# A hybrid decoder trunk on one core: how the second mixer's attention is ordered on TensorE

## The chip, the cores and the metric

One core of one Trainium2 chip runs the whole program. The metric is the device time of one execution in microseconds (us); three runs of the kernel before gave 1995.99 to 1997.3, the median is 1996.11.

## The reference, cut to what matters

Two layers, each a token mixer, a layer norm, a channel mixer of experts (PEER), a layer norm and a gate. Layer 0 mixes with an SSD, layer 1 with causal attention. The sequence has 256 tokens and one key block of 256, so the block selection of the reference selects nothing and what is left is plain causal attention with a linear position term, 16 heads of 64:

```python
logit_own = (jnp.einsum('hqd,hkd->hqk', qb, k_own).astype(f32) * scale
             - slopes[:, None, None] * dist[None])
logit_own = jnp.where((o_pos[None, :] <= t[:, None])[None], logit_own, -jnp.inf)
...
probs = jax.nn.softmax(
    jnp.concatenate([logit_sel.reshape(H, MOBA_Q_BLOCK, n_sel), logit_own], axis=-1), axis=-1)
...
        + jnp.einsum('hqk,hkd->hqd', p_own, v_own))
```

Its output goes through `w_out`, then `x = layer_norm(alpha * x + mix, ...)`, then the experts.

## The kernel before, in words

Four stages follow each other: `ssd`, `peer(0)`, `moba`, `peer(1)`. The change is in `moba` alone (and in two helpers).

Two kinds of matmul appear. **Dense** ones are products with weights. A weight chunk of 512 KB is loaded by SP's queue into `raw`, ACT casts a high part (line 113) and DVE subtracts to get a low part (line 114, `split`); `chunk` does the three. `mm3` (line 138) then issues three matmuls in the rounded format for each tile. `stationary` makes a query or key block: 8 tiles, 24 matmuls of 256 columns. `moving` makes the output projection: per chunk two halves of the tokens, 12 matmuls of 512 columns. There are four buffers for raw and four for split chunks. **Plain** ones are full fp32 matmuls: scores, transposes, values.

PSUM has three pools: `mm` (2 banks, queries and keys), `acc` (4 banks, long accumulations) and `aux` (2 banks, all the small things).

`moba` loops over eight head pairs. `query(j)` (line 558) and `key(j)` (565) make 128 rows for the two heads of pair j, head 0 on partitions 0 to 63, head 1 on 64 to 127. ACT copies the query into `qz`, a buffer per head that is zero on the other head's partitions (lines 539, 540, 563), so that a score matmul (line 583) can run over all 128 partitions of the key. Then, in `attend`:

- `scores(h2)`: two matmuls per head, for the two token blocks (128 and 256 keys); DVE adds the position term (line 586) and takes the maxima (588);
- `weights`: DVE scales the maxima (591), ACT takes four exponentials with their sums (595), DVE the reciprocals (597);
- `turn(h2)`: DVE normalises (603), PE transposes three 128x128 blocks (605), ACT copies them to SBUF (607);
- `values`: per head three matmuls onto 64 rows of the output, that is on 64 columns of the array (615 to 617); `split` stores the result for the output projection.

`out` projects earlier pairs' results from pair 3 on. The last matmuls, the two layer norms and a projection of the per-layer input follow in `end_mixer`. There the layer norm's first DVE operation (line 182) needs the projected values of pair 7.

**The order.** The program is traced in Python order, and the framework then orders each engine's instructions: by program order among those that are ready in its own estimate, so later dense matmuls move ahead of attention steps that are still waiting. `weave` (line 40) sets the program order: main steps (query and key of the next pair, an output chunk) with side steps (the attention) between them. `after(marks)` keeps what is traced in it behind given instructions on the same engine; `pace.marks` are the load and the two split halves of the latest chunk. Each engine then runs its list in order.

The lines that the prediction speaks of are 113, 114 (splits), 138 (dense matmuls), 173 (the layer norm's transposes), 196 (its last DVE step), 563, 569 (copies of query and key), 583 to 617 (attention).

Of the kernel before, what the change touches and what calls it, by code (L numbers as in the profile page):

```python
# [7 lines left out]
F32 = mybir.dt.float32  # L8
# [4 lines left out]
OP = mybir.AluOpType  # L13
AX = mybir.AxisListType.X
# [3 lines left out]
P = 128  # L18
T = 256
D = 1024  # L20
KD = D // P
# [36 lines left out]
class Net:  # L58
# [76 lines left out]

    def mm3(self, out, lhs, rhs, start, stop):
        for i, (a, b) in enumerate(SPLIT):
            self.nc.tensor.matmul(out, lhs(a), rhs(b), start=start and i == 0, stop=stop and i == 2)  # L138

    def stationary(self, out, hl, m=P):  # L140
        for k in range(KD):
            self.mm3(out, lambda a: hl[:, a, k * m:(k + 1) * m], lambda b: self.xT[:, b, k, :],
                     k == 0, k == KD - 1)

    def halves(self, out, hl):
        o = out.rearrange("p (b t) -> p b t", b=2)
# [386 lines left out]
    def moba(self):  # L533
        nc, dram = self.nc, self.dram
        with self.tc.tile_pool(name="moba", bufs=1) as pool:
            self.pool = pool
            alibi = pool.tile([P, 2, T], F32, name="alibi")
            v = pool.tile([P, 2, D], F32, name="v")
            qz = pool.tile([P, 2, 2, T], F32, name="qz")
            nc.gpsimd.memset(qz, 0.0)  # L540
            at = {}
            ks = {}

            def value(h):
                if h == 0:
                    acc, hls = self.head
                    for kp in range(4):
                        self.moving(acc[1], hls[kp], self.xk(kp, 1), kp == 0, kp == 3)
                else:
                    acc = [self.acc() for _ in range(2)]  # L550
                    for kp in range(4):
                        hl = self.chunk(dram["w_v"][h * 4 + kp])
                        for tb in range(2):
                            self.moving(acc[tb], hl, self.xk(kp, tb), kp == 0, kp == 3)
                for tb in range(2):
                    nc.scalar.copy(v[:, tb, h * 512:(h + 1) * 512], acc[tb])

            def query(j):
                pq = self.mm()
                self.stationary(pq[:, :T], self.chunk(dram["w_qk"][2 * j]))  # L560
                for h2 in range(2):
                    r = slice(64 * h2, 64 * h2 + 64)
                    nc.scalar.copy(qz[r, j % 2, h2, :], pq[r, :T])

            def key(j):
                pk = self.mm()
                self.stationary(pk[:, :T], self.chunk(dram["w_qk"][2 * j + 1]))
                ks[j] = self.tl([P, T], "k", 2)
                nc.scalar.copy(ks[j], pk[:, :T])

            def attend(j):
                s = {}

                def scores(h2):
                    if h2 == 0:
                        s["lg"] = self.tl([P, 2, 2, T], "lg", 2)
                        s["mx"] = self.tl([P, 2, 2], "mx", 2)
                        s["sm"] = self.tl([P, 2, 2], "sm", 2)
                    slope = 2.0 ** (-8.0 * (2 * j + h2 + 1) / 16)
                    psc = self.aux().rearrange("p (b s) -> p b s", b=2)  # L580
                    for tb in range(2):
                        w = (tb + 1) * P
                        nc.tensor.matmul(psc[:, tb, :w], qz[:, j % 2, h2, tb * P:w], ks[j][:, :w], start=True, stop=True)
                    for tb in range(2):
                        w = (tb + 1) * P
                        nc.vector.scalar_tensor_tensor(s["lg"][:, h2, tb, :w], alibi[:, tb, :w], 8.0 * slope,
                                                       psc[:, tb, :w], op0=OP.mult, op1=OP.add)
                        nc.vector.tensor_reduce(s["mx"][:, h2, tb:tb + 1], s["lg"][:, h2, tb, :w], AX, OP.max)

                def weights():  # L590
                    nc.vector.tensor_scalar(s["mx"], s["mx"], -0.125, None, op0=OP.mult)
                    for h2 in range(2):
                        for tb in range(2):
                            l = s["lg"][:, h2, tb, :(tb + 1) * P]
                            nc.scalar.activation(l, l, AF.Exp, bias=s["mx"][:, h2, tb:tb + 1], scale=0.125,
                                                 accum_out=s["sm"][:, h2, tb:tb + 1])
                    nc.vector.reciprocal(s["sm"], s["sm"])

                def turn(h2):
                    pt = self.aux()[:, :384].rearrange("p (b t) -> p b t", b=3)  # L600
                    for tb in range(2):
                        l = s["lg"][:, h2, tb, :(tb + 1) * P]
                        nc.vector.tensor_scalar(l, l, s["sm"][:, h2, tb:tb + 1], None, op0=OP.mult)
                    for b, (tb, sb) in enumerate(((0, 0), (1, 0), (1, 1))):
                        nc.tensor.transpose(pt[:, b, :], s["lg"][:, h2, tb, sb * P:(sb + 1) * P], self.ident)
                    s["pt", h2] = self.tl([P, 3, P], "pt", 3)
                    nc.scalar.copy(s["pt", h2], pt)

                def values():
                    po = self.aux()[:, :T].rearrange("p (b t) -> p b t", b=2)  # L610
                    for h2 in range(2):
                        r = slice(64 * h2, 64 * h2 + 64)
                        cs = slice(j * P + 64 * h2, j * P + 64 * h2 + 64)
                        pt = s["pt", h2]
                        nc.tensor.matmul(po[r, 0], v[:, 0, cs], pt[:, 0], start=True, stop=True)
                        nc.tensor.matmul(po[r, 1], v[:, 0, cs], pt[:, 1], start=True, stop=False)
                        nc.tensor.matmul(po[r, 1], v[:, 1, cs], pt[:, 2], start=False, stop=True)
                    if j % 2 == 0:
                        at[j // 2] = self.tl([P, 2, 2, T], "at", 2, F32R)
                    a = at[j // 2]  # L620
                    self.split(a[:, 0, j % 2], a[:, 1, j % 2], po.rearrange("p b t -> p (b t)"))

                return [lambda: scores(0), lambda: scores(1), weights, lambda: turn(0), lambda: turn(1), values]

            lhs = lambda kp, tb: lambda a, k: at[kp][:, a, k, tb * P:(tb + 1) * P]
            last = []

            def out(kp, h):
                hl = self.chunk(dram["w_mo"][kp * 2 + h])
                if kp >= 2:  # L630
                    last.append((h, kp, hl))
                    return
                for tb in range(2):
                    self.moving(oacc[tb][h], hl, lhs(kp, tb), kp == 0, False)

            value(0)
            with self.after(self.pace.marks):
                nc.sync.dma_start(alibi, dram["consts"][:, C_ALIBI:].rearrange("p (b s) -> p b s", b=2))
            value(1)
            query(0)  # L640
            key(0)
            oacc = self.accs()
            for j in range(8):
                main = []
                if j < 7:
                    main += [lambda: query(j + 1), lambda: key(j + 1)]
                if j >= 3:
                    kp, h = divmod(j - 3, 2)
                    main.append(lambda: out(kp, h))
                self.weave(main, attend(j))  # L650
                if j == 4:
                    gb = pool.tile([P, 2, D], F32, tag="ac", bufs=4, name="gb")
                    with self.after(self.pace.marks):
                        self.load_gb(gb, 2)
                        x = pool.tile([P, 2, D], F32, name="x")
                        nc.sync.dma_start(x, self.x_m)
                if j == 6:
                    self.ple_load(1, pool)
            out(2, 1)
            out(3, 0)  # L660
            out(3, 1)
            dump = pool.tile([P, D], F32, tag="lg", bufs=2, name="dump")
            self.end_mixer(1, oacc, x, gb, dump, pool, last, lhs)
# [398 lines left out]
```

## Time and profile before

| | before |
|---|---|
| median of 3 runs | 1996.11 us |
| the profiled execution | 1996.32 us, span 1994.4 us |
| TensorE busy | 1977.0 us, 99% of the span |
| VectorE, ScalarE busy | 78%, 57% |
| TensorE clock | full speed in all of the 40 slices |

The profile is of one execution. A busy share counts time in which an engine has an instruction running; matmuls overlap at their ends, so what a stretch of them costs is best read from the start of one group to the start of the next in the timeline. There a row gives the start, the duration, the engine, the line, the operation, the tiles and the number of merged instructions. An fp32 matmul shows as two MATMUL records (a transpose as one).

### The profile page before, as it was taken

Reading aid. Unit: us, or ns where it says so; the run is one execution under the profiler, and the core shown is the slowest. Engines: PE = TensorE matmul, PEld = TensorE weight load, DVE = VectorE, ACT = ScalarE, POOL = GpSimd, SP = SyncE. Lnnn points to the kernel's source line nnn. Section 1 sums busy time; section 2 is a strip of 40 time slices with the busy share of each in tenths; the row PEclk is TensorE's granted clock in tenths of the full one; section 3 lists DMA queues with packets and bytes.
Section 4 is the critical chain, followed back from the end, with each engine's and each line's share of the span. In section 5 each row is a group of like instructions: output and inputs, shape, how many; then the busy total and the mean of one; then the engine's idle time right before and its main releaser. Section 6 shows DMA issues by size and latency. Waiting matters only on the chain.

```text
span 1994.4 us, 33756 instructions
## 1 busy us (share of the span) xinstructions
PE 1977.0 (99%) x12658; PEld 1706.0 (86%) x12658; DVE 1549.8 (78%) x3050; ACT 1138.1 (57%) x1920; POOL 135.4 (7%) x159
## 2 busy tenths in 40 slices
PE   9999999999999999999999999999999999999999
PEld 8988898888888888888889889888888888888887
DVE  8786658998888998866765665899887889886675
ACT  7754556677556444445635645667756554445563
POOL 0001001111111000000000000111111100000000
PEclk9999999999999999999999999999999999999999
DMA  7446668888787545666735455888877755566672
GB/s 285 159 137 212 209 183 231 225 221 244 215 217 211 186 167 179 229 213 205 247 134 208 143 188 175 235 226 216 242 217 220 213 187 174 169 221 223 203 250 65
DMA packets 121155, 403.01 MB, mean 202 GB/s; under 512 B 13440, under 2 KB 14368, under 8 KB 119328
## 3 DMA queue, kind: packets, MB, share of 16 engines
q1 hardware_dynamic: 102560, 367.29, 55.4%
q0 software_dynamic: 18432, 33.56, 9.9%
q8 instruction: 100, 1.64, 0.3%
q14 instruction: 63, 0.52, 0.1%
HBM read 360.92 MB, written 6.32 MB: 184 GB/s over the span
## 4 chain that ended last, share of the span: by engine, by line
PE 85%; issue 7%; DVE 5%; ACT 2%; POOL 1%; DMA 1%; SPq 0%; POOLq 0%; ACTq 0%; DVEq 0%
PE acc L138 38%; PE acc L149 21%; PE acc L150 11%; PE mm L138 8%; PE aux L848 3%; DVE hl L114 1%; PE aux L696 1%; PE mm L378 1%; ACT hl L113 0%; PE aux L463 0%; PE mm L173 0%; DVE act L732 0%; PE mm L291 0%; DVE act L733 0%; DVE act L735 0%
## 5 line engine op out<-in xcount | busy, mean ns | idle before, releaser
L114 DVE TENSOR_TENSOR hl<-raw,hl 128x1024 fp32r<-128x1024 f32 x624 | 757.8, 1220 | 246.9 <-ACT hl L113 243.1
L149 PE MATMUL acc<-xT,hl 128*128 128x512 f32 x2048 | 722.4, 397 | 0.0
L138 PE MATMUL acc<-hl,w 128*128 128x512 f32 x3024 | 695.4, 391 | 0.0
L113 ACT CAST hl<-raw 128x1024 fp32r<-128x1024 f32 x626 | 658.3, 1054 | 39.5 <-PE acc L138 17.8
L138 PEld LDWEIGHTS acc<-hl,w 128*128 128x128 f32 x3024 | 565.5, 188 | 116.4
L150 PE MATMUL acc<-xT,hl 128*128 128x256 f32 x2048 | 573.9, 280 | 0.4 <-DVE hl L114 0.4
L149 PEld LDWEIGHTS acc<-xT,hl 128*128 128x128 f32 x2048 | 384.8, 188 | 88.6
L150 PEld LDWEIGHTS acc<-xT,hl 128*128 128x128 f32 x2048 | 387.4, 189 | 1.1 <-DVE hl L114 1.1
L113 ACT CAST w<-act 128x256 fp32r<-128x256 f32 x252 | 102.2, 407 | 344.5 <-PE acc L138 344.4
L138 PE MATMUL mm<-xT,hl 128*128 128x256 f32 x1968 | 256.4, 287 | 0.8 <-DVE xT L114 0.7
L138 PEld LDWEIGHTS mm<-xT,hl 128*128 128x128 f32 x1968 | 242.3, 192 | 5.0 <-issue 2.3
L814 ACT COPY act<-acc 128x256 f32<-128x256 f32 x256 | 96.2, 376 | 254.2 <-PE acc L150 254.2
L114 DVE TENSOR_TENSOR w<-act,w 128x256 fp32r<-128x256 f32 x252 | 106.7, 423 | 78.5 <-ACT w L113 78.2
L818 POOL DMA_DIRECT2D act<-low x128 | 110.5, 863 | 758.5 <-ACT low L815 619.4
L855 DVE SCALAR_TENSOR_TENSOR act<-aux,act 128x256 f32<-128x256 f32 x256 | 90.7, 417 | 9.9 <-PE aux L848 9.9
L815 ACT COPY low<-acc 128x256 f32<-128x256 f32 x256 | 98.2, 384 | 0.0
L839 DVE TENSOR_TENSOR a<-oh,r 128x512 f16<-128x512 f16 x256 | 96.5, 419 | 0.0
L833 DVE TENSOR_TENSOR oh<-iota,r 128x1024 f16<-128x1024 f16 x128 | 87.5, 684 | 0.0
L848 PEld LDWEIGHTS <-oh 128*128 128x128 f16 x2048 | 63.3, 98 | 13.4 <-issue 13.4
L848 PE MATMUL aux<-a,oh 128*128 128x64 f16 x2048 | 70.9, 194 | 0.0
L805 ACT ACTIVATE act<-act 128x1024 f32<-128x1024 f32 x64 | 69.0, 1078 | 0.8 <-DMA act<-low 0.8
L193 POOL TENSOR_TENSOR ln_s<-ln_s,mhalf 128x1 f32<-128x1 f32 x8 | 4.4, 549 | 874.3 <-DVE ln_s L192 874.3
(220 smaller groups left out, 1336.0 us busy)
## 6 DMA issues: line engine op xcount, KB each, us to landing
raw<-in_u SPq DMA_DIRECT2D x256, 512.0 KB, 4.4
raw<-in_v SPq DMA_DIRECT2D x256, 512.0 KB, 4.3
act<-low POOLq DMA_DIRECT2D x128, 256.0 KB, 5.5
raw<-in_w_q SPq DMA_DIRECT2D x32, 512.0 KB, 4.4
raw<-in_w_xbc SPq DMA_DIRECT2D x24, 512.0 KB, 4.3
raw<-in_w_z SPq DMA_DIRECT2D x16, 512.0 KB, 3.3
raw<-in_w_so SPq DMA_DIRECT2D x16, 512.0 KB, 3.4
raw<-in_w_pg SPq DMA_DIRECT2D x16, 512.0 KB, 4.6
```

The source lines that it names most:

```text
L113: a = self.nc.scalar.copy(hi, src)
L114: b = (lo_on or self.nc.vector).tensor_tensor(lo, src, hi.bitcast(F32), op=OP.subtract)
L138: self.nc.tensor.matmul(out, lhs(a), rhs(b), start=start and i == 0, stop=stop and i == 2)
L149: self.nc.tensor.matmul(o, hl[:, 0, c], self.xT[:, :, k, :], start=k == 0, stop=False)
L150: self.nc.tensor.matmul(out[:, :T], hl[:, 1, c], self.xT[:, 0, k, :], start=False, stop=k == KD - 1)
L814: nc.scalar.copy(act[e // 32][:, e % 32, :], pe[:, :T])
L815: copied = nc.scalar.copy(cur["low"][:, e % 2, :], pe[:, T:]).ins
L818: nc.gpsimd.dma_start(both, cur["low"], accum_op=OP.add)
L833: nc.vector.tensor_tensor(pairs(oh2), every(self.iota, P), twins(i2T, P), op=OP.is_equal)
L839: nc.vector.tensor_tensor(pairs(a2[:, k]), pairs(oh1), twins(g2[:, k], 64), op=OP.mult)
L848: nc.tensor.matmul(pg[:, t, :], oh2[:, t], a2[:, k, t], start=k == 0, stop=k == 1)
L855: nc.vector.scalar_tensor_tensor(v, pg[:, :, 32 * a:32 * a + 32].rearrange("p t e -> p e t"), 2.0 ** -12, v, op0=OP.mult, op1=OP.mult)
```

## The change

Order and shape of the attention steps. The query is no longer padded with zeros: one copy of 128 partitions, and a score matmul runs over the 64 partitions of its head, with the two heads alternating. Scores of both heads go into two auxiliary banks at once. The normalising of both heads becomes one `tensor_tensor` per token block. The six transposes stand together: five of them are held behind the first. The values stand together, heads alternating, in a bank of `mm`, and the next pair's scores are held behind the last of them. The second half of a query's matmuls (at pair 6, which has no query left, an output chunk) is held behind the transposes. Queries run two pairs ahead, keys one.

```diff
-    def stationary(self, out, hl, m=P):
+    def stationary(self, out, hl, m=P, late=()):
         for k in range(KD):
-            self.mm3(out, lambda a: hl[:, a, k * m:(k + 1) * m], lambda b: self.xT[:, b, k, :],
-                     k == 0, k == KD - 1)
+            with self.after(late if k >= KD // 2 else ()):
+                self.mm3(out, lambda a: hl[:, a, k * m:(k + 1) * m], lambda b: self.xT[:, b, k, :],
+                         k == 0, k == KD - 1)
...
-            qz = pool.tile([P, 2, 2, T], F32, name="qz")
-            nc.gpsimd.memset(qz, 0.0)
+            qs = {}
...
-            def query(j):
+            def query(j, late=()):
                 pq = self.mm()
-                self.stationary(pq[:, :T], self.chunk(dram["w_qk"][2 * j]))
-                for h2 in range(2):
-                    r = slice(64 * h2, 64 * h2 + 64)
-                    nc.scalar.copy(qz[r, j % 2, h2, :], pq[r, :T])
+                self.stationary(pq[:, :T], self.chunk(dram["w_qk"][2 * j]), late=late)
+                qs[j] = self.tl([P, T], "q", 2)
+                nc.scalar.copy(qs[j], pq[:, :T])
...
-                    for tb in range(2):
-                        w = (tb + 1) * P
-                        nc.tensor.matmul(psc[:, tb, :w], qz[:, j % 2, h2, tb * P:w], ks[j][:, :w], start=True, stop=True)
...
+                    psc = [self.aux().rearrange("p (b s) -> p b s", b=2) for _ in range(2)]
+                    with self.after(held):
+                        for tb in range(2):
+                            w = (tb + 1) * P
+                            for h2 in range(2):
+                                r = slice(64 * h2, 64 * h2 + 64)
+                                nc.tensor.matmul(psc[h2][:, tb, :w], qs[j][r, tb * P:w], ks[j][r, :w], start=True, stop=True)
...
                     for tb in range(2):
-                        l = s["lg"][:, h2, tb, :(tb + 1) * P]
-                        nc.vector.tensor_scalar(l, l, s["sm"][:, h2, tb:tb + 1], None, op0=OP.mult)
...
+                        l = s["lg"][:, :, tb, :(tb + 1) * P]
+                        nc.vector.tensor_tensor(l, l, s["sm"][:, :, tb, None].to_broadcast([P, 2, (tb + 1) * P]), op=OP.mult)
+
+                def turns():
+                    pt = [self.aux()[:, :384].rearrange("p (b t) -> p b t", b=3) for _ in range(2)]
+                    held = ()
+                    for h2, b in ((0, 2), (0, 1), (0, 0), (1, 2), (1, 1), (1, 0)):
+                        tb, sb = (b + 1) // 2, b // 2
+                        with self.after(held):
+                            ins = nc.tensor.transpose(pt[h2][:, b, :], s["lg"][:, h2, tb, sb * P:(sb + 1) * P], self.ident).ins
+                        held = held or (ins,)
...
+                    return (ins,)
+
+                def close(then):
+                    po = self.mm()[:, :T].rearrange("p (b t) -> p b t", b=2)
+                    held = ()
+                    for n, (tb, sb) in enumerate(((0, 0), (1, 0), (1, 1))):
+                        for h2 in (1, 0):
...
+                            with self.after(held):
+                                ins = nc.tensor.matmul(po[r, tb], v[:, sb, cs], s["pt", h2][:, n], start=sb == 0, stop=sb == tb).ins
+                            held = held or (ins,)
...
+                    then((ins,))
...
+            heads = [attend(j) for j in range(8)]
+            heads[0][0](())
+            query(1)
             for j in range(8):
-                main = []
                 if j < 7:
-                    main += [lambda: query(j + 1), lambda: key(j + 1)]
+                    key(j + 1)
+                with self.after(self.pace.marks):
+                    heads[j][1]()
+                    turned = heads[j][2]()
                 if j >= 3:
-                    kp, h = divmod(j - 3, 2)
-                    main.append(lambda: out(kp, h))
-                self.weave(main, attend(j))
+                    out(*divmod(j - 3, 2), late=turned if j >= 6 else ())
+                if j < 6:
+                    query(j + 2, turned)
+                with self.after(self.pace.marks):
+                    heads[j][3](heads[j + 1][0] if j < 7 else lambda held: None)
```

## Rows read from the trace of the kernel before

**Rows 1.** The page, part 1: busy us, share of the span, instructions of each engine.
```profile
PE 1977.0 (99%) x12658; PEld 1706.0 (86%) x12658; DVE 1549.8 (78%) x3050; ACT 1138.1 (57%) x1920; POOL 135.4 (7%) x159
```

**Rows 2.** Windows, first values to last values: PE, PEld, DVE, ACT, POOL busy, clock, DMA share, GB/s.
```profile
1081.12:1153.82 72.70, 71.89 (x506) 63.55 (x506) 49.94 (x125) 45.02 (x113) 0.00 (x0) 1.00 0.49 171
```

**Rows 3.** PE's timeline after the mixer: start, us, instructions, idle before and releaser.
```profile
1163.61 0.65 PE L173 MATMUL mm<-ident,x 128*128 128x128 f32 x4 [2.06 <-DVE x L196]
```

**Rows 4.** PE's timeline, end of pair 4 to pair 6.
```profile
1124.07 1.48 PE L583 MATMUL aux<-k,qz 128*128 128x128 f32 x8
1125.20 3.23 PE L138 MATMUL mm<-xT,hl 128*128 128x256 f32 x24
1128.26 2.94 PE L138 MATMUL acc<-hl,at 128*128 128x512 f32 x12
1131.03 0.40 PE L138 MATMUL mm<-xT,hl 128*128 128x256 f32 x2
1131.56 0.33 PE L605 MATMUL aux<-ident,lg 128*128 128x128 f32 x1
...
1132.47 1.31 PE L138 MATMUL mm<-xT,hl 128*128 128x256 f32 x9
1133.71 0.43 PE L615 MATMUL aux<-pt,v 128*64 128x128 f32 x2
1133.98 0.27 PE L616 MATMUL aux<-pt,v 128*64 128x128 f32 x1
1133.99 0.32 PE L615 MATMUL aux<-pt,v 128*64 128x128 f32 x1
...
1134.47 0.38 PE L617 MATMUL aux<-pt,v 128*64 128x128 f32 x2
1134.79 1.58 PE L138 MATMUL mm<-xT,hl 128*128 128x256 f32 x11
1136.21 1.48 PE L583 MATMUL aux<-k,qz 128*128 128x128 f32 x8
```

**Rows 5.** PE's timeline, pair 7.
```profile
1152.47 0.27 PE L605 MATMUL aux<-ident,lg 128*128 128x128 f32 x1
...
1153.82 0.43 PE L615 MATMUL aux<-pt,v 128*64 128x128 f32 x2
...
1155.00 5.17 PE L138 MATMUL acc<-hl,at 128*128 128x512 f32 x21
```

**Rows 6.** DVE's timeline, pair 5.
```profile
1124.93 0.62 DVE L586 SCALAR_TENSOR_TENSOR lg<-alibi,aux 128x128 f32<-128x128 f32 x2 [1.46 <-PE aux L583]
...
1127.04 1.22 DVE L114 TENSOR_TENSOR hl<-raw,hl 128x1024 fp32r<-128x1024 f32 x1
...
1131.21 1.01 DVE L603 TENSOR_SCALAR lg<-lg,sm 128x128 f32<-128x128 f32 x4
```

**Rows 7.** DVE's timeline, pair 7.
```profile
1149.66 0.17 DVE L591 TENSOR_SCALAR mx<-mx 128x4 f32<-128x4 f32 x1
...
1151.98 1.01 DVE L603 TENSOR_SCALAR lg<-lg,sm 128x128 f32<-128x128 f32 x4
```

**Rows 8.** Groups by line and form, second mixer: count, busy us, mean ns, idle before.
```profile
L114 DVE TENSOR_TENSOR at<-aux,at 128x256 fp32r<-128x256 f32 x8 | 3.4, 424 | 7.1 <-ACT at L113 7.0
...
L114 DVE TENSOR_TENSOR pT<-raw,pT 128x512 fp32r<-128x512 f32 x1 | 0.7, 693 | 0.5 <-ACT pT L113 0.5
```

**Rows 9.** One line: ACT's copy of the keys, ns min/median/max, first and last start.
```profile
L569 ACT COPY k<-mm x8: 372/372/373, 1068.2 to 1140.6; 128x256 f32<-128x256 f32 x8
```

**Rows 10.** PE's timeline, pair 0.
```profile
1070.90 1.48 PE L583 MATMUL aux<-k,qz 128*128 128x128 f32 x8
...
1079.42 0.33 PE L605 MATMUL aux<-ident,lg 128*128 128x128 f32 x1
...
1081.12 0.43 PE L615 MATMUL aux<-pt,v 128*64 128x128 f32 x2 [0.18 <-ACT pt L607]
```

**Rows 11.** DVE's timeline, pair 0.
```profile
1071.76 0.62 DVE L586 SCALAR_TENSOR_TENSOR lg<-alibi,aux 128x128 f32<-128x128 f32 x2 [0.96 <-PE aux L583]
```

More of the change, by code (lines that the diff above doesn't have):

```diff
@@ L137, in mm3 @@
         for i, (a, b) in enumerate(SPLIT):
-            self.nc.tensor.matmul(out, lhs(a), rhs(b), start=start and i == 0, stop=stop and i == 2)
-    def stationary(self, out, hl, m=P):
+            self.last_mm = self.nc.tensor.matmul(out, lhs(a), rhs(b), start=start and i == 0, stop=stop and i == 2).ins
+    def stationary(self, out, hl, m=P, late=()):
         for k in range(KD):
-            self.mm3(out, lambda a: hl[:, a, k * m:(k + 1) * m], lambda b: self.xT[:, b, k, :],
-                     k == 0, k == KD - 1)
+            with self.after(late if k >= KD // 2 else ()):
+                self.mm3(out, lambda a: hl[:, a, k * m:(k + 1) * m], lambda b: self.xT[:, b, k, :],
+                         k == 0, k == KD - 1)
     def halves(self, out, hl):
@@ L572, in attend, with scores @@
                 s = {}
[L574 to L580, printed above, removed]
-                    for tb in range(2):
-                        w = (tb + 1) * P
-                        nc.tensor.matmul(psc[:, tb, :w], qz[:, j % 2, h2, tb * P:w], ks[j][:, :w], start=True, stop=True)
[L584 to L588, printed above, removed]
+                def scores(held):
+                    s["lg"] = self.tl([P, 2, 2, T], "lg", 2)
+                    s["mx"] = self.tl([P, 2, 2], "mx", 2)
+                    s["sm"] = self.tl([P, 2, 2], "sm", 2)
+                    psc = [self.aux().rearrange("p (b s) -> p b s", b=2) for _ in range(2)]
[5 more added lines that the diff above has]
+                                nc.tensor.matmul(psc[h2][:, tb, :w], qs[j][r, tb * P:w], ks[j][r, :w], start=True, stop=True)
+                    for h2 in range(2):
+                        slope = 2.0 ** (-8.0 * (2 * j + h2 + 1) / 16)
+                        for tb in range(2):
+                            w = (tb + 1) * P
+                            nc.vector.scalar_tensor_tensor(s["lg"][:, h2, tb, :w], alibi[:, tb, :w], 8.0 * slope,
+                                                           psc[h2][:, tb, :w], op0=OP.mult, op1=OP.add)
+                            nc.vector.tensor_reduce(s["mx"][:, h2, tb:tb + 1], s["lg"][:, h2, tb, :w], AX, OP.max)
                 def weights():
@@ L597, in weights @@
                     nc.vector.reciprocal(s["sm"], s["sm"])
-                def turn(h2):
-                    pt = self.aux()[:, :384].rearrange("p (b t) -> p b t", b=3)
                     for tb in range(2):
-                        l = s["lg"][:, h2, tb, :(tb + 1) * P]
-                        nc.vector.tensor_scalar(l, l, s["sm"][:, h2, tb:tb + 1], None, op0=OP.mult)
[L604 to L607, printed above, removed]
@@ L609, in values @@
-                def values():
-                    po = self.aux()[:, :T].rearrange("p (b t) -> p b t", b=2)
-                    for h2 in range(2):
[L612 to L617, printed above, removed]
+                        l = s["lg"][:, :, tb, :(tb + 1) * P]
@@ new lines, in weights @@
+                        nc.vector.tensor_tensor(l, l, s["sm"][:, :, tb, None].to_broadcast([P, 2, (tb + 1) * P]), op=OP.mult)
[7 more added lines that the diff above has]
+                        held = held or (ins,)
+                    for h2 in range(2):
+                        s["pt", h2] = self.tl([P, 3, P], "pt", 3)
+                        nc.scalar.copy(s["pt", h2], pt[h2])
+                    return (ins,)
@@ new lines, in close @@
+                def close(then):
[3 more added lines that the diff above has]
+                        for h2 in (1, 0):
+                            r = slice(64 * h2, 64 * h2 + 64)
+                            cs = slice(j * P + 64 * h2, j * P + 64 * h2 + 64)
+                            with self.after(held):
+                                ins = nc.tensor.matmul(po[r, tb], v[:, sb, cs], s["pt", h2][:, n], start=sb == 0, stop=sb == tb).ins
+                            held = held or (ins,)
@@ L621, in values, with out @@
                     self.split(a[:, 0, j % 2], a[:, 1, j % 2], po.rearrange("p b t -> p (b t)"))
-                return [lambda: scores(0), lambda: scores(1), weights, lambda: turn(0), lambda: turn(1), values]
+                    then((ins,))
+                return scores, weights, turns, close
             lhs = lambda kp, tb: lambda a, k: at[kp][:, a, k, tb * P:(tb + 1) * P]
             last = []
-            def out(kp, h):
+            def out(kp, h, late=()):
                 hl = self.chunk(dram["w_mo"][kp * 2 + h])
@@ L632, in out @@
                     return
-                for tb in range(2):
-                    self.moving(oacc[tb][h], hl, lhs(kp, tb), kp == 0, False)
+                with self.after(late):
+                    for tb in range(2):
+                        self.moving(oacc[tb][h], hl, lhs(kp, tb), kp == 0, False)
             value(0)
```

## The prediction, made before the change had run

> **What bounds the kernel now.** I read the page's busy shares first: TensorE (PE) is busy 99% of the span [rows 1], so a change counts only through what PE must execute or wait for. Then the windows by stage: from the first values to the last ones of the second mixer 72.70 us pass, 71.89 of them with PE busy; VectorE (DVE) and ScalarE (ACT) are busy 49.94 and 45.02 us there and the DMA engines half the time [rows 2], so neither they nor the loads bound this stage now. But PE is full here because dense matmuls fill whatever the attention leaves: behind it hangs a serial chain (scores, DVE, exponentials on ACT, DVE, transposes, copy on ACT, values), and right after the mixer PE is idle: 2.06 us before a transpose that waits for the layer norm [rows 3]. The layer norm needs the last values. So the number to forecast is when the last values end; what comes earlier there reaches the end of the kernel, what PE saves alone does not.
>
> **The pieces that PE executes, per head pair.** Below, V is the start of a pair's values.
>
> Dense: 24 query or key matmuls go from 1125.20 to 1128.26, 3.06 us; 0.19 of it belongs to what stood before (next paragraph), so 2.88, or 0.12 each. An output chunk of 12 takes 2.77 (1128.26 to 1131.03 where the next begins) by the same view, 0.23 each [rows 4]. Their number is not changed.
>
> Scores: a plain matmul shows as two passes. Eight passes start at 1124.07, the first dense one at 1125.20, and the 24 that follow take 0.19 too long: 1.31 us [rows 4], for twelve times 128 columns, 0.11 each. After the change two heads lie on separate halves of the rows. No row of before shows two row halves. The bounds are 1.31 (no overlap) and half of it, 0.65 (full overlap). I take 0.65, since the nearest rows, the values, which lie on two column halves, do overlap: passes of the two heads start 0.01 us apart (1133.98, 1133.99), where each needs 0.11 [rows 4].
>
> Leaving a half array costs something: the last two passes of the values take 0.32 us until the dense matmul at 1134.79, 0.10 more than two passes, and the eleven dense after it take 1.42 until 1136.21 instead of 1.32, 0.10 again [rows 4]. So 0.2 us per switch back. The change has three switches per pair where there were two: into columns, from columns to rows, from rows to the whole array. The added one costs 0.2 x 8 = 1.6 us; if rows switch for nothing, 0. I take 0.2. The Trainium skill speaks against the change here: "TensorEngine Tiling (Array Packing)", Key Properties, says that changing the tiling mode drains TensorE. The rows agree for columns; for rows nothing in this trace shows it.
>
> Values: 1.18 us from 1153.82 to 1155.00, plus the 0.10 after it, 1.28 [rows 5]. The second head starts late there. With the heads alternating, six slots of 0.11 and a slow first pass (0.05: the first two passes take 0.27 from 1133.71 to 1133.98 [rows 4]) give 0.70, plus 0.20 for leaving: 0.90. The bounds are that and 1.28; I take 0.90, a gain of 0.38, since the overlap is there now for the passes that can.
>
> Transposes: 1131.56 to 1132.47 with two dense ones inside, 0.67 and 0.08 lost on the dense behind [rows 4]. Without the dense inside 0.70. Gain 0.05.
>
> If PE alone counted, a pair would gain 0.38 + (1.31 - 0.65 - 0.2 = 0.46) + 0.05, about 0.9, and eight pairs 7.2 us.
>
> **What the change does to the chain.** Now scores of the next pair follow the values of this one, the transposes wait for the normalising of both heads, and half a query (12 matmuls) is held between transposes and values. So one pair cannot start before the last has ended, and a cycle from V to V is a sum of latencies:
>
> (1) V to the first scale of the next pair on DVE. V 0.80, 0.10 switch, scores 0.65, hand-over 0.21 (before: scores at 1124.07, DVE at 1124.93, 0.86 for one head of 0.65 [rows 4, 6]): 1.76.
>
> (2) From there to the transposes, call it c. DVE's eight scales and maxima of both heads take 2.11 (1124.93 to 1127.04) [rows 6]; from the small scale at 1149.66 to the first transpose at 1152.47 it is 2.81 [rows 5, 7]; with 0.03 between, 4.95 undisturbed. Now the normalising becomes two operations with a broadcast operand, and the first transpose needs both: nearest rows 424 ns for 256 elements and 693 for 512 [rows 8], 1.1 together, against 0.35 from the normalising's start to the first transpose now (1131.21 to 1131.56) [rows 4, 6]: 0.7 later. So c is at least 5.65. The upper end: pair 5, where a 1.22 us split of the weights slid in between on DVE (at 1127.04) [rows 6], took 1124.93 to 1131.56, 6.63, so 7.33. I take 6.3: the middle, 6.5, less half of the 0.37 us query copy on ACT that goes (two of 64 partitions become one of 128; the key's copy is 372 ns [rows 9]).
>
> (3) Transposes 0.70, then the held half query, 12 x 0.12 = 1.44: 2.14. This hides the copy of the transposes: transposes to values takes 2.15 in pair 5 and 1.35 in pair 7 [rows 4, 5], where 0.15 is added since the values now begin with the head copied last. For pair 6 the held work is an output chunk, 2.77; pair 7 has none, 1.50.
>
> The sum: five cycles of 1.76 + 6.3 + 2.14 = 10.2, 51.0; pair 6 1.76 + 6.3 + 0.70 + 2.77 = 11.53; pair 7, with c at 5.65 since no weights come in there (as now), 1.76 + 5.65 + 1.50 = 8.91. Together 71.44 against 72.70 [rows 2]: -1.26.
>
> The start: the first scores stand behind the whole second query now (1070.90) although the first key's copy began at 1068.2 and took 0.37 [rows 10, 9]. In the new order they come ahead of it, at about 1068.8. Then 0.86 to DVE, 7.66 to the transposes (1071.76 to 1079.42, the load of a table in it) plus 0.7, plus 2.14: V at 1080.16 instead of 1081.12 [rows 10, 11]: -0.96.
>
> The end: the last values take 0.38 less. Total -0.96 - 1.26 - 0.38 = -2.6. Against the profiled execution's 1996.32 that gives 1993.7; the median of the runs is 0.21 below that execution, so 1993.5.
>
> Costed at nothing, with cover: the memset of the padded queries on GpSimd, idle here, goes. The loads are the same, one query earlier on SP; the queue is half idle [rows 2], and if it were late the next dense block would wait. The values take a bank of the dense matmuls' pair instead of an auxiliary one; the next key needs the other, whose copy (0.37) has the values and scores (1.6 us) as cover. Where PE runs dry: in the cycles of pairs 1 and 2 there are 24 + 12 dense matmuls, 4.3 us, ahead of the transposes for c less the 0.2 of hand-over, so up to 1.8 us of waiting for the normalising, unless the next key is pulled forward as dense work is now. Behind the waiting transposes stand the held half query, the values and the next scores, and the next cycle waits for those. The order to expect it in is not fixed; if it is not pulled, pairs 3 to 5 (8.5 us of dense each) take 11.0 instead of 10.2: +2.4.
>
> **Rivals.** *The dense work covers the chain.* If the splits stay out of it (DVE has nothing for 2 us during the exponentials, 1149.66 to 1151.98 [rows 7], wide enough for one), c is 5.65 and six cycles lose another 0.65: -6.5, 1989.6; PE's own limit, -7.2, is 1988.9. For: pair 7 shows it. Against: pair 5, with weights to split, does not. Chance 0.33.
>
> *The joined chain gets the split every time*: place, DVE between the maxima of both heads and the reciprocal; c 7.33 in all seven, +1.03 x 6 + 1.68 on the forecast: +5.3 in all, 2001.4 as a median. It makes the kernel slower from c = 7.4 in six cycles alone, or 7.15 in all seven. For: DVE's share of the stage is 69% and the normalising now sits wholly on the path. Against: it needs every pair disturbed. Chance 0.13.
>
> *The rows don't overlap* (the change doesn't do what it says): scores 1.31 plus the switch, 0.66 more for eight pairs, +5.3 on the chain: 1998.8. Against: the columns overlap. Chance 0.07. The Trainium skill, "TensorE: Matmul & The Clock Gate", Part 3, says that small matmuls on different row groups run concurrently; by it the forecast stands; no row here shows it.
>
> **The numbers.** The forecast, 1993.5, has 0.47. A measurement of this kernel tells about 0.2% from no change, 4.0 us: faster is below 1992.1, slower above 2000.1. The forecast lies inside, save 0.02 of it (c below 6.07 is faster); with the rows that don't overlap, "same" has 0.52. Faster: 0.33 + 0.02. Slower: 0.13. The range goes from PE's own limit to near the second rival's price, 1989.0 to 2001.0, and leaves out most of that rival's upper half and a few hundredths below.
>
> **What would show it.** Right: a score group of eight passes over 0.65 to 0.9 us, values of 0.80, DVE's first scale about 1.8 us after V, transposes 5.7 to 7.3 us behind that, PE waiting there for the normalising in pairs 1 and 2, and V to V near 10.2 us. Wrong: passes of the two heads 0.11 apart and never closer (rows don't overlap); no wait ahead of the transposes and the layer norm over 6 us earlier (cover holds); c above 7.2 with a split in each pair (slower); or idle time after the mixer that takes up what came earlier.

## The result, and the profile after

The changed kernel took 2009.61 us (median of 6 runs, 2007.02 to 2012.08) beside 1998.07 for the kernel before: ratio 1.0058, 95% interval 1.0046 to 1.0070. It is slower by 11.5 us, outside the range of the prediction. Its runs differ more than those of before, and in step with the mean granted clock: 0.994 in the longest run, 0.997 in the shortest. The profiled execution is the longest, 2012.08.

The windows of the kernel after (columns as in [rows 2], the granted clock ahead of the last two): the stage from the first values to the last, a stretch of it, and one behind the mixer.

```profile
1083.13:1167.96 84.83, 75.67 (x533) 63.78 (x533) 49.11 (x110) 42.77 (x108) 0.00 (x0) 0.94 0.40 140
...
1092.51:1095.89 3.38, 3.38 (x19) 3.16 (x19) 0.00 (x0) 0.90 (x2) 0.00 (x0) 0.60 0.26 99
1185.08:1189.00 3.92, 3.92 (x19) 3.92 (x20) 3.23 (x4) 0.66 (x2) 0.00 (x0) 0.53 0.27 97
```

The stage takes 84.83 us where it took 72.70 [rows 2]. PE was busy for all but 0.8 us of it; now it is idle for 9.2. And the clock, at full speed throughout before, is granted at 0.94 over the stage and at 0.60 in the stretch, that is, mostly at the lower of its two levels, 1.2 GHz. Against the profiled execution of before (1996.32) the kernel takes 15.8 us more; 14.1 of them are there when the last values start (1167.96 for 1153.82 [rows 2]), and 1.6 come from the 3.9 us behind the mixer at a clock of 0.53 (the 96 dense matmuls that begin there take 13.23 us, 11.61 in the kernel before). So the stage is where the time goes.

PE's timeline of the kernel after, pairs 0 to 2 (start, us, instructions, idle before and releaser):

```profile
1079.37 1.37 PE L610 MATMUL aux<-ident,lg 128*128 128x128 f32 x6 [1.91 <-DVE lg L602]
1080.38 2.81 PE L138 MATMUL mm<-xT,hl 128*128 128x256 f32 x12
1083.13 0.88 PE L625 MATMUL mm<-pt,v 128*64 128x128 f32 x12
1083.93 0.93 PE L583 MATMUL aux<-k,q 64*128 64x128 f32 x8
1084.79 4.57 PE L138 MATMUL mm<-xT,hl 128*128 128x256 f32 x36
1092.51 0.88 PE L610 MATMUL aux<-ident,lg 128*128 128x128 f32 x6 [3.16 <-DVE lg L602]
1093.12 2.84 PE L138 MATMUL mm<-xT,hl 128*128 128x256 f32 x12
1095.89 1.21 PE L625 MATMUL mm<-pt,v 128*64 128x128 f32 x12
...
1105.57 0.85 PE L610 MATMUL aux<-ident,lg 128*128 128x128 f32 x6 [0.33 <-DVE lg L602]
...
1107.77 0.88 PE L625 MATMUL mm<-pt,v 128*64 128x128 f32 x12
```

The same view, pairs 5 to 7:

```profile
1130.84 0.88 PE L625 MATMUL mm<-pt,v 128*64 128x128 f32 x12
...
1138.44 1.20 PE L138 MATMUL acc<-hl,at 128*128 128x512 f32 x4 [0.68 <-DVE hl L114]
1140.58 1.15 PE L610 MATMUL aux<-ident,lg 128*128 128x128 f32 x6 [0.94 <-DVE lg L602]
...
1144.23 0.94 PE L625 MATMUL mm<-pt,v 128*64 128x128 f32 x12
...
1153.62 0.84 PE L610 MATMUL aux<-ident,lg 128*128 128x128 f32 x6 [3.14 <-DVE lg L602]
1154.22 4.58 PE L138 MATMUL acc<-hl,at 128*128 128x512 f32 x12
1158.73 0.88 PE L625 MATMUL mm<-pt,v 128*64 128x128 f32 x12
...
1167.96 0.88 PE L625 MATMUL mm<-pt,v 128*64 128x128 f32 x12
```

What the prediction said of the pieces is there. The scores of both heads take 0.86 us from 1083.93 to the next dense matmul at 1084.79 (1.13 before, 1124.07 to 1125.20 [rows 4]; what they cost on the dense ones behind is taken up below), the values 0.80 (1083.13 to 1083.93), the six transposes 0.61 (1092.51 to 1093.12). But PE waits 1.91, 3.16 and 3.14 us before the transposes of pairs 0, 1 and 6, always for the normalising (line 602), and after each of these waits the dense matmuls run at half speed: the 12 held ones take 2.75 (1080.38 to 1083.13) and 2.77 (1093.12 to 1095.89) instead of 1.44, the 12 of 512 columns at 1154.22 4.51 instead of 2.77. Pair 5 gets there with two shorter waits, 0.68 and 0.94, with four matmuls between: 3.65 from its transposes to its values. Pair 2 waits 0.33 and takes 2.20 for the same (1105.57 to 1107.77).

Why the normalising is late: DVE's timeline in pair 1 (pair 0's values start at 1083.13), and ACT's below it.

```profile
1084.64 1.23 DVE L114 TENSOR_TENSOR hl<-raw,hl 128x1024 fp32r<-128x1024 f32 x1 [4.29 <-ACT hl L113]
...
1086.12 0.61 DVE L588 SCALAR_TENSOR_TENSOR lg<-alibi,aux 128x128 f32<-128x128 f32 x2
...
1088.33 0.17 DVE L593 TENSOR_SCALAR mx<-mx 128x4 f32<-128x4 f32 x1
```
```profile
1083.56 1.05 ACT L113 CAST hl<-raw 128x1024 fp32r<-128x1024 f32 x1
...
1088.28 1.05 ACT L113 CAST hl<-raw 128x1024 fp32r<-128x1024 f32 x1
1089.23 0.40 ACT L597 ACTIVATE lg<-lg,mx 128x128 f32<-128x128 f32 x1
```

The held half query ends exactly where the values begin. Its weight buffer comes free there (there are four, so the chunk four places later takes it), ACT casts that chunk (1083.56), and DVE's low part of it (1084.64, 1.23 us) stands ahead of the result's split and of the scales. The first scale comes 2.99 us after the values instead of the 1.76 forecast. ACT does the same once more when the key ends: a cast at 1088.28 ahead of the first exponential (1089.23), although the maxima were ready at 1088.5.

### The profile page after: what moved, and what is told of

It is laid out like the page before. It is cut to its first block, busy times and chain, and to the rows that moved or that the text cites. A ratio compares the mean times of both kernels' runs of the same rounds, so it can differ in the third digit from the quotient of the medians.

```text
span 2010.0 us, 33722 instructions
## 1 busy us (share of the span) xinstructions
PE 1979.8 (98%) x12658; PEld 1703.7 (85%) x12658; DVE 1549.4 (77%) x3034; ACT 1135.6 (56%) x1912; POOL 135.0 (7%) x158
## 5 line engine op out<-in xcount | busy, mean ns | idle before, releaser
L866 PEld LDWEIGHTS <-oh 128*128 128x128 f16 x2048 | 63.3, 98 | 13.4 <-issue 13.4
```

What stands on the lines that cost most here:

```text
L866: nc.tensor.matmul(pg[:, t, :], oh2[:, t], a2[:, k, t], start=k == 0, stop=k == 1)
```

## The experiments

The theory after this reading: the loop from values to values is a serial chain, the holds put the weight splits into it, PE runs dry, and the clock falls after the waits. A shared quantity for all kernels is the start of the last values, in the profiled execution of each:

| kernel | median us | ratio to before (95%) | last values start, us |
|---|---|---|---|
| before | 1998.07 | 1 | 1153.82 |
| changed | 2009.61 | 1.0058 (1.0046 to 1.0070) | 1167.96 |
| e1_twice: keys of three pairs issued twice | 2007.04 | 1.0049 (1.0032 to 1.0065) | 1163.29 |
| e2_nohold: no holds behind the transposes | 1997.89 | 1.0002 (0.9992 to 1.0012) | 1153.41 |
| e3_rows128: scores on 128 rows | 2012.39 | 1.0076 (1.0059 to 1.0092) | 1169.28 |
| e5_split_behind: splits behind the softmax | 1999.21 | 1.0007 (0.9998 to 1.0017) | 1156.06 |
| e8_outhold: only pair 6's hold kept | 2000.29 | 1.0014 (1.0005 to 1.0024) | 1156.58 |
| e10_split_free6: e5 without pair 6's hold | 1997.85 | 1.0002 (0.9992 to 1.0011) | 1153.18 |
| e7_before64: before, scores on 64 rows | 2001.34 | 1.0020 (1.0010 to 1.0029) | 1157.23 |
| e4_ahead: scores two pairs ahead | 1989.94 | 0.9961 (0.9947 to 0.9976) | 1144.32 |
| e6_ahead128: e4, scores on 128 rows | 1993.13 | 0.9980 (0.9971 to 0.9990) | 1147.98 |
| e9_ahead_nohold: e4 without holds | 1987.71 | 0.9948 (0.9931 to 0.9965) | 1144.41 |

The kernel before, run beside the experiments, had medians of 1997.1 to 1997.5.

**e1, work laid into the waits.**

```diff
-                self.stationary(pk[:, :T], self.chunk(dram["w_qk"][2 * j + 1]))
+                hl = self.chunk(dram["w_qk"][2 * j + 1])
+                for _ in range(2 if j in (1, 2, 7) else 1):
+                    self.stationary(pk[:, :T], hl)
```

> This kernel is the changed one with the 24 matmuls of the keys of pairs 1, 2 and 7 issued twice (the second pass overwrites the first with the same sums): 72 more dense matmuls, 8.6 us of TensorE work, placed where TensorE now waits for the normalising of pairs 0, 1 and 6 (2.1, 3.3 and 3.3 us). Theory (the waits come from too little dense work ahead of the transposes, and the clock falls to 1.2 GHz after them): the added work lies in the waits, all but some 0.8 us of it costs nothing, the stretches at half clock behind these three waits go (about 5 us), and the time falls from 2009.6 to 2004 to 2006. Rival (the clock has nothing to do with the waits, or the transposes wait for TensorE itself): the time rises by 0.8 to 8.6 us, to 2010.5 to 2018, and the half-clock stretches stay.

PE's timeline of e1, pair 1:

```profile
1081.40 0.88 PE L627 MATMUL mm<-pt,v 128*64 128x128 f32 x12
...
1083.06 6.84 PE L138 MATMUL mm<-xT,hl 128*128 128x256 f32 x55
1090.09 0.85 PE L612 MATMUL aux<-ident,lg 128*128 128x128 f32 x6 [0.18 <-DVE lg L604]
1090.69 2.27 PE L138 MATMUL mm<-xT,hl 128*128 128x256 f32 x17
1092.89 0.88 PE L627 MATMUL mm<-pt,v 128*64 128x128 f32 x12
```

2007.04. With 8.6 us more work for PE the kernel is not slower; the ratio falls from 1.0058 to 1.0049, and the two intervals overlap, so the medians alone don't show a gain. The profile does: the cycle of pair 1, values to values, is 11.49 us instead of 12.76, with 24 more matmuls in it, the wait is 0.18 and the 17 matmuls behind the transposes take 2.20, full speed. So the wait was real idle time, and the half clock behind it came from the idling, not from the plain matmuls. It missed its range by 1 us: pair 5, where nothing was added, still fell to half speed, and so did the stretch after the mixer.

**e2, no holds.**

```diff
-                    out(*divmod(j - 3, 2), late=turned if j >= 6 else ())
+                    out(*divmod(j - 3, 2), late=())
...
-                    query(j + 2, turned)
+                    query(j + 2)
```

> This kernel is the changed one without the hold of half a query (and of pair 6's output chunk) behind the transposes. Theory (too little dense work in a serial loop): 1.4 us more cover ahead of the transposes in pairs 0 and 1 and 2.8 us in pair 6, but the copy of the transposes (0.9 to 1.5 us) then stands open ahead of the values in each pair; the loop stays a sum of latencies, so 2003 to 2010, with the clock down less often. Rival (the hold is the cause): back to the kernel before, 1998, or below it.

PE's timeline of e2, pair 1, and DVE's below it:

```profile
1081.05 0.88 PE L625 MATMUL mm<-pt,v 128*64 128x128 f32 x12 [0.91 <-ACT pt L614]
...
1082.71 6.01 PE L138 MATMUL mm<-xT,hl 128*128 128x256 f32 x48
1088.79 0.85 PE L610 MATMUL aux<-ident,lg 128*128 128x128 f32 x6
...
1090.95 0.88 PE L625 MATMUL mm<-pt,v 128*64 128x128 f32 x12
```
```profile
1082.81 0.62 DVE L588 SCALAR_TENSOR_TENSOR lg<-alibi,aux 128x128 f32<-128x128 f32 x2
```

1997.89, the kernel before again: the rival's number. All of the loss hangs on the holds. But not by their 1.44 us of cover alone. Here the first scale comes 1.76 us after the values, the transposes 5.98 behind it, with no split in between: the query now ends before the transposes (48 dense matmuls ahead of them, 36 with the hold), and the next split is done when the scales come. And the hold bought nothing: from the transposes to the values it is 2.16 us here (1088.79 to 1090.95), with a wait of 0.55 in it, against 2.20 in a pair of the changed kernel where the held half query fills it at full speed.

**e3, the rows alone.**

```diff
-                                nc.tensor.matmul(psc[h2][:, tb, :w], qs[j][r, tb * P:w], ks[j][r, :w], start=True, stop=True)
+                                nc.tensor.matmul(psc[h2][:, tb, :w], qz[:, j % 2, h2, tb * P:w], ks[j][:, :w], start=True, stop=True)
```

> This kernel is the changed one with the scores on all 128 rows again (padded queries), all else kept. Theory (the scores on row halves work, 0.86 us a pair with the switch back against 1.31; they stand in the serial chain): 0.4 to 0.5 us more in each of eight pairs, +3 to +4, 2012.5 to 2014. Rival (row halves and their mode switches are what costs): the time falls, below 2007.

2012.39, 2.8 us over the changed kernel, 3.6 by the two ratios, just under the expected range. The two intervals overlap, so the size is better read from the profiles: the cycles of pairs 3 and 4, values to values and at full clock, take 12.00 us each, 11.54 and 11.53 in the changed kernel. The rows on halves are a gain in the changed kernel too; they are not what made it slow.

**e5, the splits moved out of the chain, the holds kept.** `weights` returns the last exponential and the last normalising step; `done` is that pair of the iteration before.

```diff
-                self.stationary(pk[:, :T], self.chunk(dram["w_qk"][2 * j + 1]))
+                self.stationary(pk[:, :T], self.chunk(dram["w_qk"][2 * j + 1], after=done))
...
-                    query(j + 2, turned)
+                    query(j + 2, turned, done)
+                done = soft
```

> This kernel is the changed one, holds and all; only the splits of the weight chunks on ScalarE and VectorE are held behind the softmax of the pair before (a chunk of iteration j behind the last exponential and the normalising of pair j-1). Theory (the held half query ends just where the values begin, frees its weight buffer there, and the next chunk's split then stands in the chain on VectorE and ScalarE): from the values to VectorE's first scale 1.8 to 1.9 us instead of 2.8, from there to the transposes 5.7 to 6.0 instead of 6.6 to 7.0, the wait of pair 1 falls from 3.3 to 1.4 to 1.8 us, the waits of pairs 2 to 4 go, the clock falls less often: 1999 to 2003. Rival (only the 12 held matmuls matter, not where splits land): within 2 us of the changed kernel, 2008 to 2011.

PE's timeline of e5, pair 1 (pair 0's values end at 1079.72, where the scores start) and one line of pair 6, and DVE's, pair 1, below it:

```profile
1079.72 0.93 PE L583 MATMUL aux<-k,q 64*128 64x128 f32 x8
1080.58 4.56 PE L138 MATMUL mm<-xT,hl 128*128 128x256 f32 x36
1086.65 0.85 PE L611 MATMUL aux<-ident,lg 128*128 128x128 f32 x6 [1.51 <-DVE lg L602]
1087.25 1.67 PE L138 MATMUL mm<-xT,hl 128*128 128x256 f32 x12
1088.86 0.88 PE L626 MATMUL mm<-pt,v 128*64 128x128 f32 x12
...
1140.50 0.78 PE L138 MATMUL acc<-hl,at 128*128 128x512 f32 x2 [2.52 <-ACT hl L113]
```
```profile
1080.68 0.62 DVE L588 SCALAR_TENSOR_TENSOR lg<-alibi,aux 128x128 f32<-128x128 f32 x2
...
1086.42 2.35 DVE L114 TENSOR_TENSOR hl<-raw,hl 128x1024 fp32r<-128x1024 f32 x2
```

1999.21: with every hold in place, moving the splits gives back 10 of the 11.5 us. The scales start 0.10 after the scores, as in e2, the transposes 5.97 behind them (1080.68 to 1086.65), the splits (1086.42) come after the normalising. The wait is 1.51 us, and behind it the 12 held matmuls take 1.61, full speed. So the theory holds, and the rival (only the 12 matmuls matter) falls: the same 12 are held here. Three details don't fit the expectation or the account. Pair 2 waits 1.51 too, where its wait was to go. In pair 6 PE waits 2.52 for ACT's cast of its output chunk (1140.50), which this kernel holds back, and the clock falls behind it. And some 2 of the 10 us lie in pair 0, where splits stand in the chain without any hold too: its values start at 1078.92 here, at 1081.05 in e2 and at 1083.13 in the changed kernel.

**e8 and e10, pair 6 by itself.** e8 is the changed kernel with `query(j + 2)` instead of `query(j + 2, turned)`; e10 is e5 without `late` on `out`.

> The changed kernel without the hold of half a query, but with pair 6's output chunk still held behind the transposes. Theory (each hold takes away dense work where there is little): pairs 0 to 5 as without holds, pair 6 waits 2 to 3 us with the clock down after it: 2000 to 2003, between the kernel without holds (1997.9) and the changed one (2009.6). Rival (pair 6's hold costs nothing): 1997 to 1999.

> The changed kernel with the splits behind the softmax (1999.2) and pair 6's output chunk no longer held; the half queries stay held. Theory (two faults in all: splits that land in the chain, and pair 6's hold): the 2.8 us wait and the half clock of pair 6 go, 1996 to 1998. Rival (pair 6 waits for its chain anyway): within 0.7 us of 1999.2.

PE's timeline of e8, pair 6:

```profile
1143.81 0.85 PE L610 MATMUL aux<-ident,lg 128*128 128x128 f32 x6 [1.99 <-DVE lg L602]
1144.41 3.02 PE L138 MATMUL acc<-hl,at 128*128 128x512 f32 x12
```

2000.29 against 1997.89 without it: 2.4 us. The intervals of the two just overlap; in the profiles the cycle of pair 6 takes 2.07 longer (12.89 us for 10.82 in e2), with a wait of 1.99 before its transposes, which is the hold's price by this profile. In e10 taking it away gives 1.4, at the weak end of what was expected, and the intervals overlap; in the profiles e5's 2.52 of waiting in pair 6 and the half clock behind it are gone, and the last values start 2.9 earlier. After e8's wait of 1.99 the clock stays up, against the expectation (the 12 matmuls of 512 columns behind it show 3.02, where 12 at full speed show 2.94 [rows 4]).

**e7, one part of the change on the kernel before.** The scores of both heads in one step, on 64 rows, one copy of the query; weaving and all else as before.

> The kernel before, with this one part of the change: the scores of both heads in one step on 64 rows each, one query copy. Its weaving, transposes and values stay. Theory (TensorE is full there and the chain has cover): the 0.46 us a pair is gained, less 1 us or so that joining the heads costs in the chain: 1994 to 1996. Rival (joining the heads' scores by itself starves TensorE): above 1999.

PE's timeline of e7 from pair 7's scores to its first transpose, and the same of the kernel before, whose first transpose starts at 1152.47 [rows 5]:

```profile
1149.26 0.92 PE L581 MATMUL aux<-k,q 64*128 64x128 f32 x4
1150.10 0.72 PE L138 MATMUL acc<-hl,at 128*128 128x512 f32 x2
...
1155.89 0.27 PE L605 MATMUL aux<-ident,lg 128*128 128x128 f32 x1
```
```profile
1146.40 0.92 PE L583 MATMUL aux<-k,qz 128*128 128x128 f32 x4
1146.98 0.81 PE L138 MATMUL acc<-hl,at 128*128 128x512 f32 x2
```

2001.34: 4 us slower, a miss. The step was one in the program, but nothing held it together: in five of eight pairs two to eight dense matmuls came between the heads, presumably because an auxiliary bank came free later for the second. Then nothing overlaps, and each head pays the switch: 0.84 us to the next dense matmul (1149.26 to 1150.10) against 0.58 for a head on all rows (1146.40 to 1146.98). In pair 7 both kernels execute the same matmuls between the first score and the first transpose, and e7 takes 6.63 us for them, the kernel before 6.07. Five pairs lose some 0.56 each so, three gain 0.36 (below): 1.7 of the 4 us. Where the rest comes from is open; it was not tried further.

**e4, e6 and e9, the chain given a whole cycle.** No instruction is changed against the changed kernel, only the order:

```diff
-            heads[0][0](())
-            query(1)
+            begin(0)(())
+            query(1)
+            key(1)
+            begin(1)(())
+            query(2)
             for j in range(8):
-                if j < 7:
-                    key(j + 1)
+                if j < 6:
+                    key(j + 2)
                 with self.after(self.pace.marks):
-                    heads[j][1]()
                     turned = heads[j][2]()
...
-                if j < 6:
-                    query(j + 2, turned)
+                if j < 5:
+                    query(j + 3, turned)
                 with self.after(self.pace.marks):
-                    heads[j][3](heads[j + 1][0] if j < 7 else lambda held: None)
+                    heads[j][3](begin(j + 2) if j < 6 else lambda held: None)
```

`begin(j)` is the scores and then the softmax of pair j. e6 has these scores on 128 rows (as e3), e9 no `late`.

> This kernel keeps every instruction of the changed one but puts scores and softmax two pairs ahead: the scores of pair j+2 stand behind the values of pair j, queries run three and keys two pairs ahead. Theory (the chain from scores to transposes is longer than the dense work of one pair; what TensorE executes did get cheaper, about 0.9 us a pair): the chain has a whole cycle of cover, waits ahead of the transposes under 0.5 us, clock at full speed throughout, and the time falls below the kernel before by 4 to 7 us: 1991 to 1994. Rival (the new pieces are dearer in themselves, or half clock comes from the plain stretches): above the kernel before, 2000 or more.

> The kernel with scores two pairs ahead, but its scores on all 128 rows (padded queries). Theory (there TensorE is full, so the 0.4 to 0.5 us a pair that row halves save counts in full): 3 to 4 us over that kernel's 1989.9, 1993 to 1994. Rival (with the chain covered, the score's width is hidden beside other work): within 1 us of it.

> The kernel with scores two pairs ahead, without any hold behind the transposes. Theory (a hold hurts only where the chain has no cover): within 1.5 us of 1989.9. Rival (holds cost in themselves): 1985 to 1988; or they are needed to cover the copy of the transposes: 1992 or more.

PE's timeline of e4 from pair 0's values to pair 1's transposes, then DVE's, then a window over the attention (the first scores start at 1069.12, the last values at 1144.32):

```profile
1086.29 0.88 PE L625 MATMUL mm<-pt,v 128*64 128x128 f32 x12 [0.45 <-ACT pt L614]
1087.09 0.93 PE L583 MATMUL aux<-k,q 64*128 64x128 f32 x8
1087.95 3.13 PE L138 MATMUL mm<-xT,hl 128*128 128x256 f32 x24
1090.92 0.82 PE L610 MATMUL aux<-ident,lg 128*128 128x128 f32 x6
```
```profile
1087.48 1.22 DVE L114 TENSOR_TENSOR hl<-raw,hl 128x1024 fp32r<-128x1024 f32 x1 [0.71 <-ACT hl L113]
...
1088.96 0.61 DVE L588 SCALAR_TENSOR_TENSOR lg<-alibi,aux 128x128 f32<-128x128 f32 x2
```
```profile
1068.60:1143.80 75.20, 74.27 (x595) 65.36 (x594) 55.13 (x124) 48.94 (x125) 0.00 (x0) 1.00 0.53 179
```

1989.94, 7.5 us under the kernel before and 1 us below the expected range. The split still lands ahead of the scales (1087.48; the first scale 2.67 us after the values), and it costs nothing: these scales belong to a pair whose transposes are a cycle away. PE waits 0.45 for the copy of the transposes, nowhere in the mixer for the normalising, and the clock is granted at 1.00. With the chain covered the row halves are worth 3.2 us by the medians (e6, 1993.13) and 3.7 by the start of the last values, what PE's own sum gave, 0.46 x 8 = 3.7. Against the kernel before, whose heads don't alternate, they are worth less: scores and the 24 dense matmuls behind them take 3.83 us here (1087.09 to 1090.92) and 4.19 there (1124.07 to 1128.26 [rows 4]), 0.36 a pair.

Without holds it is 1987.71 (e9), 9.4 us or 0.52% under the kernel before and the lowest median of all. That the holds cost 2 us here too, the rival's number, is not shown: the intervals of e4 and e9 overlap, and in the profiles the last values start at the same time (1144.32, 1144.41). What differs there lies behind the mixer, where the layer norm's first transposes start at 1155.02 in e4 and at 1153.97 in e9; why is open.

## Why the prediction was wrong

The pieces that PE executes were right in their sum: values 0.80 for 0.90, scores 0.95 for 0.85 (0.86 to the next dense matmul and 0.09 on the 24 behind, e4), transposes 0.61 for 0.70. The rival in which the rows don't overlap is out: in e7 one head alone takes what both take together here, 0.84 for 0.86. Two rules were cited from the Trainium skill: that small matmuls on different row groups run concurrently ("TensorE: Matmul & The Clock Gate", Part 3), and that changing the tiling mode drains TensorE ("TensorEngine Tiling (Array Packing)", Key Properties). The first agrees with these 0.84 and 0.86, and of the second the rows show that the switch has a cost, the 0.09 behind the scores. Between e6 and e4 the gain of the rows shows nearly in full. That the saving would be given back in a serial chain was right too; the sizes of the chain were not.

*Step (1), 1.76 us from the values to the first scale, failed.* Undisturbed it is exactly that (1.76 in e2, and in pair 7, where no split is due), but the changed kernel takes 2.99 in pair 1 and 2.93 to 3.03 in pairs 2 to 6. I had put the weight split into c, as an upper end, and not asked when the split becomes due: the half query that the change holds ends at the values, so its buffer is free there in every cycle. *Step (2), c, was near*: 6.39 in pair 1 (1086.12 to 1092.51), for 6.3. Values to transposes came to 9.38 in pair 1, 9.68 in pair 2, 9.74 in pair 5 and 9.39 in pair 6, for the forecast's 8.06 and the 9.09 of the rival that proved nearest, the split in every cycle. Over seven cycles that is some 8.5 us, 7.2 of them in step (1).

*"Unless the next key is pulled forward"*, named as open and priced at 2.4, is a part of these 8.5, which the split alone doesn't explain. The key wasn't pulled: in pairs 2 to 4 36 dense matmuls of 256 columns and 12 of 512 stand ahead of the transposes and 12 behind, and PE waits only 0.33 us, so these cycles of 11.53 to 11.88 for the forecast's 10.2 are nearly full of PE's own work. e5, with the splits out of the chain, still takes 11.27 and 11.26 in pairs 3 and 4; and in pair 4 of e2 the first scale comes 2.94 us after the values, behind a split, without any wait on PE. So some 3 of the 8.5 us would be there without the splits, and the splits hurt in pairs 1, 5 and 6 (4.3 us), where PE has too little to do. By the program an unfinished query holds one of the two banks of `mm`, and the values want the other; that this is why the key stays behind is not tested.

*Step (3), 2.14 us from transposes to values, left the clock out.* It is 2.20 in the pairs at full speed, 3.38 in pair 1 and 3.65 in pair 5, and 5.11 instead of 3.47 in pair 6: 4.8 us. I priced waits of up to 1.8 us in pairs 1 and 2 by their length alone; pair 2 waited 0.33, but pair 1 waited 3.16, and what stood behind that ran at half speed. These 4.8 and the 8.5 make up the 13.4 that the stage took beyond the forecast's 71.44. Ahead of it the first values came 3.0 late (1083.13 for 1080.16): 1.6 of that is again half speed, 3.76 instead of 2.14 from pair 0's transposes (1079.37) to its values; for the rest the first scores start 0.8 later than forecast, and a split stands ahead of pair 0's first scale too.

Behind the mixer the same term is missing. What comes earlier there was to reach the end of the kernel, but e2's last values start 0.41 earlier than those of the kernel before, and the 96 dense matmuls behind the layer norm then take 13.95 us instead of 11.61, at a granted clock of 0.81.

## What to carry to other kernels

Before holding work back to cover a later wait, ask what the held work frees when it ends, and which queue that lands in: here a buffer, hence a cast and a subtraction, in front of the step that everything waited for. In a loop that is a serial chain, filling one wait with work taken from ahead of another gained nothing here; start the chain an iteration earlier, as e4 does, and both the cover and the cheaper pieces count. And price a wait on TensorE with what runs behind it, not by its length alone.

## What the runs showed of the hardware

After waits of 3.16 and 3.14 us the six transposes still took 0.61, as at full speed, and the dense matmuls behind them ran at half speed (12 in 2.77 us instead of 1.44); in e3, after waits of 3.15 and 3.14, the transposes too were slow (1.12 and 1.17). After waits of 1.51 (e5), 1.99 (e8) and 2.52 (e3, the line below) the clock stayed up; after 1.91 in pair 0, after 0.68 and 0.94 with four matmuls between, in pair 5, and after 2.52 in e5's pair 6 it fell. So the length of one wait does not decide it alone.

PE's timeline of e3, pair 0; the granted clock is 1.00 from here to the values at 1083.24:

```profile
1081.03 0.85 PE L611 MATMUL aux<-ident,lg 128*128 128x128 f32 x6 [2.52 <-DVE lg L603]
```

Two heads of 64 rows each, alternating, take 0.86 us in fp32 until the next dense matmul, as long as one of them alone (0.84 and 0.85 in e7): they overlap. Alone on its half a head takes longer than on all rows (0.58 in the kernel before).
